# Threshold search of a sparse-attention layer: VectorE's three tiles in two streams in place of one

## The chip, the cores and the metric

The kernel runs on one core of one Trainium2 chip. The metric is device time in microseconds, taken as the median of repeated runs. A profile shows one execution, instruction by instruction. Its engines are PE (TensorE, matrix products), PEld (its weight loads), DVE (VectorE), ACT (ScalarE), POOL (GpSimd) and SP (SyncE, which issues the transfers).

## What is computed

The kernel is one decoder layer of width 1024 over 1024 tokens: a modulation of the input, one combined input projection, a mixer of sparse attention (8 heads) and causal pooling, a layer norm, and a gated feed-forward part with a second layer norm. The part that matters here is the choice of keys. An indexer gives each query a score for every earlier key, and the 256 keys of the highest score take part in that query's attention:

```
score = jnp.einsum('bqh,bqhs->bqs', w, jax.nn.relu(logits))
score = jnp.where(causal[None], score, -jnp.inf)
_, idx = lax.top_k(score, k_sel)              # k_sel = 256
...
s = jnp.where(valid[:, None], s, -jnp.inf)
p = jax.nn.softmax(s, axis=-1)
```

The queries are cut into eight tiles of 128. Tile i sees 128 (i + 1) keys, so tiles 0 and 1 take all of their keys and tiles 2 to 7 need a search for the 256th highest score.

## The kernel before

**The search.** Function `bisect` searches a list of tiles bit by bit. A score is cut into a high and a low half of 16 bits. For each of 15 bits of the high half and then 16 of the low half, a step counts, row by row, how many keys are at least a candidate, and then moves the candidate up or down by half of the last move. On VectorE (`search_v`) a step is one counting instruction per tile (a tensor_scalar that also writes out its sum; the trace calls it TENSOR_SCALAR_CACHE_REDUCE) and then two tiny instructions on one column per tile, which serve all tiles of the list at once:

```
for m, i in enumerate(tiles):
    dt = U16 if low else I16
    V.tensor_scalar(trash(i).bitcast(dt), kv[i].bitcast(dt), one(cand, m), one(base, m),
                    ALU.is_ge, ALU.add, accum_out=one(cntc, m))
V.tensor_scalar(pr, cntc, 0.0, float(1 << b), ALU.is_ge, ALU.mult)
off = -float(1 << (b - 1)) if b > 0 else -1.0
V.scalar_tensor_tensor(cand, pr, off, cand, ALU.add, ALU.add)
```

In this text these two are called the pair. Between the halves, each tile gets one more count (the keys above the high half) and a pass that builds its low keys; so a tile has 31 counts of the search and one more. After the low half each tile has a tail of passes: which keys equal the threshold, which lie below it, a scan that settles ties in order of position, and the write of the mask over the scores. `biased` then holds the tile. Tiles 4 and 3 in one list and tile 2 in another are searched by ScalarE (`search_a`, with Sign activations), with preparation and tail on VectorE. VectorE itself searches tiles 7, 6 and 5 in one list. Names in the trace: `keysD` and `keys` hold the keys, `junk` takes the counts' unused output, `colsD` the columns of VectorE's list, `colsA` those of ScalarE's.

**What sets the order.** `bisect` is a generator that yields, before each piece, the engine and a rough duration. While the projections are written out, the queues keep a clock of their own, and `fill` puts pieces of the search into an engine's queue ahead of an instruction of the main line that would otherwise leave that engine waiting by this clock; among the pieces that fit it takes the one that could start first. `need(i)` is called where attention needs tile i and advances the streams until it is masked. During the projections the order on VectorE, ScalarE and GpSimd is kept as written; after them (`pinned.clear()`) a scheduler decides, by its own estimates, what stands where on each engine.

**The stages around the change.** The index scores are accumulated on VectorE tile by tile (`score`). Then TensorE runs the pooling, key and value projections (`pair`, `pj` in the trace). Here VectorE has the search and besides it four subtractions for pooling (`u_split`, in the trace `ub<-ub,ub`; after them ScalarE writes `phi`, GpSimd `plo`, and TensorE multiplies, `po`), and eight pairs of writes of key operands (`kr<-kT`). GpSimd adds the pooling windows, rotates the keys (`rope`) and splits weights (`ws`). Then attention goes by groups of two query tiles: 7 and 6, 5 and 4, 3 and 2, 1 and 0. The query operands (`qab`) of tiles 7 and 6 are split once. For each pair of heads and each tile, a unit is: score products on TensorE (`s`), on VectorE a masked maximum per head that also adds the mask (`sm<-s,score`, CUSTOM_DVE_ANT_0 in the trace, ISA in the order below), exponentials on ScalarE, a reciprocal on VectorE (`stat`), the scaling on GpSimd (`sm<-sm,stat`), transposes on TensorE (`pT`), their copies on ScalarE and VectorE, and the products with the values (`o`). The weight blocks and the feed-forward part that follow are not touched.

Of the kernel before, what the change touches and what calls it, by code (L numbers as in the profile page):

```python
# [34 lines left out]
NEG = -3.0e38  # L35
NOT_TAKEN = -(2.0 ** 100)
TILES_A = [[4, 3], [2]]
TILES_V = [7, 6, 5]
PIN = "VAG"
AHEAD = 2  # L40
AHEAD_SMALL = 2
# [140 lines left out]
def decoder_layer_kernel(  # L182
# [8 lines left out]
    V, A, G, T, SP = (Queue(tc, e, n, pinned, times) for e, n in  # L191
                      ((nc.vector, "V"), (nc.scalar, "A"), (nc.gpsimd, "G"), (nc.tensor, "T"), (nc.sync, "S")))
# [13 lines left out]
    def buf(where, off, n, name, dt=F32):  # L206
        return nc.alloc_sbuf_tensor_at(f"{name}_{where}{off}", [P, n], dt, offset=area[where] + 4 * off).ap()
# [419 lines left out]
    def junkd(i):  # L627
        return junks.get(i, junk7)[:, 0 : P * (i + 1)]
# [4 lines left out]
    junkA = buf("T", 1664, 384, "junkA").bitcast(BF16)  # L633
    junkB = buf("X", 7360, 192, "junkB").bitcast(BF16)
    colsD = buf("X", 8576, 64, "colsD")
    keys = {2: kA[:, 0:192], 3: kA[:, 192:448], 4: k4, 5: k5, 6: kD[:, 0:448], 7: kD[:, 448:960]}
    keys = {i: kw.bitcast(I16) for i, kw in keys.items()}

# [2 lines left out]
    def bisect(tiles, cols, on_act):  # L641

        nt = len(tiles)
# [6 lines left out]
        def trash(i):  # L650
            return (ja if on_act else junkd(i))[:, 0 : P * (i + 1)]

        one = lambda c, m: c[:, m : m + 1]
        w_ = lambda i: (i + 1) / 8
# [17 lines left out]
        sum_w = sum(w_(i) for i in tiles)  # L672
# [13 lines left out]
        def search_a(bits, low):  # L686

            V.memset(cand, 0.5 - float(1 << (bits - 1)))
            for b in range(bits - 1, -1, -1):
                yield "A", 0.9 * sum_w + nt  # L690
                for m, i in enumerate(tiles):
                    A.activation(trash(i), kv[i].bitcast(U16 if low else I16), AF.Sign, bias=one(cand, m),
                                 accum_out=one(cntc, m))

                for m in range(nt):
                    A.activation(one(pr, m), one(cntc, m), AF.Sign, bias=one(thr, m))
                for m in range(nt):
                    A.activation(one(cand, m), one(pr, m), AF.Identity, scale=-0.5 * float(1 << b), bias=one(cand, m))
            yield "V", 0.1
            V.tensor_scalar(cand, cand, -1.0, None, ALU.mult)  # L700
# [40 lines left out]
    streams = []  # L741

    def open_stream(*a):
        pinned.update(PIN)
        b = bisect(*a)
        streams.append([T.t, next(b), b])
        times.fill = fill

    def start(st):
        return max(st[0], queues[st[1][0]].t)  # L750

    def advance(st):
        fill, times.fill = times.fill, None
        q = queues[st[1][0]]
        try:
            st[1] = next(st[2])
        except StopIteration:
            streams.remove(st)
        st[0] = q.t
        times.fill = fill  # L760

    def need(i):
        while i not in biased:
            advance(min(streams, key=start))

    def fill(q, until):
        while True:
            todo = [st for st in streams if st[1][0] == q.name and start(st) + st[1][1] <= until + SLACK.get(q.name, 0.0)]
            if not todo:
                return  # L770
            advance(min(todo, key=start))


    n_rr = [0]
# [12 lines left out]
    for i in range(2, NT):  # L787
# [27 lines left out]
                q_evac(*qpend.pop(0))  # L815
        dg = sc[:, n - P : n]
        G.affine_select(dg, dg, pattern=[[-1, P]], compare_op=ALU.is_ge, fill=NEG, base=0, channel_multiplier=1)
    open_stream(TILES_V, colsD, False)


    SP.dma_start(pscale, pscale_in)
# [309 lines left out]
    for n_, u in enumerate(units):  # L1131
        g, pr, i = u
# [162 lines left out]
    for p in range(NFP):  # L1295
# [7 lines left out]
        for kind in DOWN_AT if "d" in sets else "g" * 7 + "u" * 7:  # L1303
            w_ = names[kind].pop(0)
# [595 lines left out]
```

## Time and profile before

| | us |
|---|---|
| median of 3 runs (1322.52 to 1326.69) | 1326.66 |
| the profiled execution | 1332.07 |
| its span, first to last instruction | 1330.0 |
| PE, DVE busy over the span | 1197.3, 1071.2 |
| ACT, POOL busy over the span | 643.3, 734.5 |

The profiled execution is one run among others and lies 5.4 us above the median; a sum is made against its own time and carried over to the median. The shares over the whole span are means over stages with different limits, so the stages are read one by one, in the windows and in the engines' order of time. A row of the time line gives the start, the duration, the engine, the line (L169 is the helper through which every instruction goes), the operation, output<-inputs, shapes and the count of instructions; in brackets stands the idle time before it and what ended that.

### The profile page before, as it was taken

Reading aid. Unit: us, or ns where it says so; the run is one execution under the profiler, and the core shown is the slowest. Engines: PE = TensorE matmul, PEld = TensorE weight load, DVE = VectorE, ACT = ScalarE, POOL = GpSimd, SP = SyncE. Lnnn points to the kernel's source line nnn. Section 1 sums busy time; section 2 is a strip of 40 time slices with the busy share of each in tenths; the row PEclk is TensorE's granted clock in tenths of the full one; section 3 lists DMA queues with packets and bytes.
Section 4 is the critical chain, followed back from the end, with each engine's and each line's share of the span. In section 5 each row is a group of like instructions: output and inputs, shape, how many; then the busy total and the mean of one; then the engine's idle time right before and its main releaser. Section 6 shows DMA issues by size and latency. Waiting matters only on the chain.

```text
span 1330.0 us, 16034 instructions
## 1 busy us (share of the span) xinstructions
PE 1197.3 (90%) x5462; PEld 933.9 (70%) x5462; DVE 1071.2 (81%) x1755; ACT 643.3 (48%) x1335; POOL 734.5 (55%) x509
## 2 busy tenths in 40 slices
PE   7979998989258997999689999999999999999996
PEld 6646676768135654788577788878787887878775
DVE  6898999999996798466687787777868787777698
ACT  3345776868735776435544333333333333333431
POOL 1392496671013355327578384755748475666848
PEclk8999998989657998899899999999999999999998
DMA  9540021311000266320021101112020101113113
GB/s 338 222 160 26 17 95 51 109 48 40 16 0 10 70 216 238 123 92 9 32 96 33 64 32 65 55 40 80 32 80 32 64 33 64 64 42 117 41 61 121
DMA packets 34903, 103.90 MB, mean 78 GB/s; under 512 B 3843, under 2 KB 3843, under 8 KB 33286
## 3 DMA queue, kind: packets, MB, share of 16 engines
q1 hardware_dynamic: 34822, 102.88, 22.5%
q8 instruction: 43, 0.70, 0.2%
q14 instruction: 38, 0.31, 0.1%
HBM read 93.42 MB, written 9.45 MB: 77 GB/s over the span
## 4 chain that ended last, share of the span: by engine, by line
PE 55%; DVE 25%; POOL 7%; issue 6%; ACT 4%; DMA 2%; SPq 0%; DVEq 0%; POOLq 0%; ACTq 0%
PE gu L169 24%; PE dn L169 14%; DVE junk_X L169 4%; PE wo L169 4%; PE pj L169 3%; DVE score_X L169 3%; PE pT L169 2%; PE s L169 2%; PE o L169 2%; PE pair L169 2%; DVE act_W L169 2%; POOL wraw_R L169 1%; DVE utmp_X L169 1%; DVE stat_C L169 1%; DVE hr_H L169 1%
## 5 line engine op out<-in xcount | busy, mean ns | idle before, releaser
L169 PE MATMUL gu<-hr_H,wblk_T 128*128 128x512 f32 (+1 forms) x924 | 216.2, 385 | 4.7 <-POOL wblk_T L169 1.9
L169 PE MATMUL gu<-hr_H,wblk_V 128*128 128x512 f32 (+1 forms) x924 | 215.2, 384 | 3.7 <-POOL wblk_V L169 1.9
L169 PEld LDWEIGHTS gu<-hr_H,wblk_T 128*128 128x128 f32 x924 | 171.0, 189 | 41.3 <-POOL wblk_T L169 3.6
L169 PEld LDWEIGHTS gu<-hr_H,wblk_V 128*128 128x128 f32 x924 | 170.1, 188 | 40.0 <-POOL wblk_V L169 3.6
L169 DVE TENSOR_TENSOR res_X<-res_X,dn 128x512 f32<-128x512 f32 (+1 forms) x253 | 158.9, 677 | 15.4 <-PE dn L169 15.3
L169 POOL TENSOR_SCALAR sm_H<-sm_H,stat_X 128x1024 f32<-128x1024 f32 (+7 forms) x64 | 58.2, 921 | 164.8 <-DVE stat_X L169 142.7
L169 POOL TENSOR_TENSOR wraw_R<-wraw_R 128x512 f32<-128x512 f32 x64 | 94.7, 1486 | 47.0 <-DVE wblk_T L169 23.7
L169 PE MATMUL pj<-ws_W,hT_H 128*128 128x512 f32 x456 | 117.4, 404 | 2.5 <-DVE const_C L169 1.7
L169 POOL TENSOR_TENSOR wraw_W<-wraw_W 128x512 f32<-128x512 f32 x60 | 86.7, 1452 | 58.0 <-DVE wblk_V L169 29.3
L169 PEld LDWEIGHTS pj<-ws_W,hT_H 128*128 128x128 f32 x456 | 84.0, 190 | 27.6 <-issue 10.1
L169 PE MATMUL dn<-wblk_T,act_W 128*128 128x512 f32 x324 | 79.7, 395 | 4.7 <-DVE act_W L169 4.7
L169 PE MATMUL dn<-wblk_V,act_W 128*128 128x512 f32 x324 | 78.6, 391 | 2.9 <-DVE act_W L169 2.5
L169 DVE TENSOR_SCALAR_CACHE_REDUCE junk_X<-keysD_T,colsD_X 128x1024 int16<-128x1024 int16 (+1 forms) x64 | 79.0, 1270 | 0.9
L169 PEld LDWEIGHTS dn<-wblk_T,act_W 128*128 128x128 f32 x324 | 60.9, 189 | 19.4 <-DVE act_W L169 6.8
L169 ACT ACTIVATE wblk_V<-wraw_R 128x512 fp32r<-128x512 f32 x56 | 35.2, 629 | 80.7 <-POOL wraw_R L169 62.2
L169 PEld LDWEIGHTS dn<-wblk_V,act_W 128*128 128x128 f32 x324 | 60.4, 188 | 17.5 <-DVE act_W L169 4.2
L169 POOL TENSOR_TENSOR ws_W<-raw_R,ws_W 128x1024 fp32r<-128x1024 f32 x17 | 43.9, 2604 | 48.9 <-ACT ws_W L169 48.9
L169 ACT ACTIVATE wblk_V<-wraw_W 128x512 fp32r<-128x512 f32 x53 | 33.1, 627 | 75.0 <-POOL wraw_W L169 56.4
L169 ACT ACTIVATE wblk_T<-wraw_W 128x512 fp32r<-128x512 f32 x56 | 35.0, 628 | 66.3 <-POOL wraw_W L169 50.2
L169 ACT ACTIVATE sm_H<-sm_H,stat_X 128x1024 f32<-128x1024 f32 (+7 forms) x64 | 49.0, 768 | 34.0 <-DVE stat_X L169 34.0
L169 ACT ACTIVATE wblk_T<-wraw_R 128x512 fp32r<-128x512 f32 x52 | 32.5, 627 | 61.2 <-POOL wraw_R L169 45.8
L169 PE MATMUL pT<-const_C,sm_H 128*128 128x128 f32 x288 | 49.3, 308 | 10.9 <-POOL sm_H L169 6.4
(297 smaller groups left out, 2796.3 us busy)
## 6 DMA issues: line engine op xcount, KB each, us to landing
wm_K<-in_wma_dram SPq DMA_DIRECT2D x16, 512.0 KB, 9.6
modraw_V<-in_wmc_dram SPq DMA_DIRECT2D x16, 512.0 KB, 4.5
wraw_R<-in_wg_dram SPq DMA_DIRECT2D x6, 1024.0 KB, 4.8
wraw_R<-in_wd_dram SPq DMA_DIRECT2D x12, 512.0 KB, 3.5
wraw_W<-in_wup_dram SPq DMA_DIRECT2D x12, 512.0 KB, 3.5
modraw_V<-in_wmg_dram SPq DMA_DIRECT2D x10, 512.0 KB, 4.6
wraw_R<-in_wup_dram SPq DMA_DIRECT2D x10, 512.0 KB, 3.6
wraw_W<-in_wg_dram SPq DMA_DIRECT2D x5, 1024.0 KB, 4.8
```

The source lines that it names most:

```text
L169: ins_ = f(*a, **k)
```

## The change

VectorE's list becomes two: tiles 7 and 6 with the columns `colsD`, and tile 5 with columns of its own, `colsE`, in a place that was free. `fill` takes, among pieces that could start at the same time, the stream of the higher tile first; `need` advances the stream that holds the tile asked for, and no longer whichever could start first, so tile 5 has to be done only when attention asks for it. ScalarE's search is handed out count by count in place of step by step, with the same stated durations in sum; its instructions are the same.

```diff
--- before.py
+++ after.py
@@ -35,7 +35,7 @@
 NEG = -3.0e38
 NOT_TAKEN = -(2.0 ** 100)
 TILES_A = [[4, 3], [2]]
-TILES_V = [7, 6, 5]
+TILES_V = [[7, 6], [5]]
 PIN = "VAG"
 AHEAD = 2
 AHEAD_SMALL = 2
@@ -633,6 +633,7 @@
     junkA = buf("T", 1664, 384, "junkA").bitcast(BF16)
     junkB = buf("X", 7360, 192, "junkB").bitcast(BF16)
     colsD = buf("X", 8576, 64, "colsD")
+    colsE = buf("X", 5312, 64, "colsE")
     keys = {2: kA[:, 0:192], 3: kA[:, 192:448], 4: k4, 5: k5, 6: kD[:, 0:448], 7: kD[:, 448:960]}
     keys = {i: kw.bitcast(I16) for i, kw in keys.items()}
 
@@ -687,10 +688,11 @@
 
             V.memset(cand, 0.5 - float(1 << (bits - 1)))
             for b in range(bits - 1, -1, -1):
-                yield "A", 0.9 * sum_w + nt
                 for m, i in enumerate(tiles):
+                    yield "A", 0.9 * w_(i) + 0.45
                     A.activation(trash(i), kv[i].bitcast(U16 if low else I16), AF.Sign, bias=one(cand, m),
                                  accum_out=one(cntc, m))
+                yield "A", 0.55 * nt
 
                 for m in range(nt):
                     A.activation(one(pr, m), one(cntc, m), AF.Sign, bias=one(thr, m))
@@ -743,7 +745,7 @@
     def open_stream(*a):
         pinned.update(PIN)
         b = bisect(*a)
-        streams.append([T.t, next(b), b])
+        streams.append([T.t, next(b), b, a[0]])
         times.fill = fill
 
     def start(st):
@@ -761,14 +763,14 @@
 
     def need(i):
         while i not in biased:
-            advance(min(streams, key=start))
+            advance(next(st for st in streams if i in st[3]))
 
     def fill(q, until):
         while True:
             todo = [st for st in streams if st[1][0] == q.name and start(st) + st[1][1] <= until + SLACK.get(q.name, 0.0)]
             if not todo:
                 return
-            advance(min(todo, key=start))
+            advance(min(todo, key=lambda st: (start(st), -max(st[3]))))
 
 
     n_rr = [0]
@@ -815,7 +817,8 @@
                 q_evac(*qpend.pop(0))
         dg = sc[:, n - P : n]
         G.affine_select(dg, dg, pattern=[[-1, P]], compare_op=ALU.is_ge, fill=NEG, base=0, channel_multiplier=1)
-    open_stream(TILES_V, colsD, False)
+    for q, tiles in enumerate(TILES_V):
+        open_stream(tiles, (colsD, colsE)[q], False)
 
 
     SP.dma_start(pscale, pscale_in)
```

What this does to VectorE's queue, at three places. A counting instruction stands here as a TENSOR_SCALAR with two outputs, `junk` and the column.

In the projections, ahead of the subtraction for pooling, VectorE has whole steps of three tiles before:

```order
L169 TENSOR_SCALAR junk_X_607,colsD_X_615<-keysD_T_610,colsD_X_615 128x1024
L169 TENSOR_SCALAR junk_X_608,colsD_X_615<-keysD_T_610,colsD_X_615 128x896
L169 TENSOR_SCALAR junk_X_609,colsD_X_615<-keys_T_612,colsD_X_615 128x768
L169 TENSOR_SCALAR colsD_X_615<-colsD_X_615 128x3
L169 SCALAR_TENSOR_TENSOR colsD_X_615<-colsD_X_615 128x3
L169 SCALAR_TENSOR_TENSOR ub_V_1220<-ub_V_1220,ub_V_1221 128x1024
```

And in the changed kernel a step of two tiles, and one of tile 5 with a pair of its own:

```order
L169 TENSOR_SCALAR junk_X_607,colsD_X_615<-keysD_T_610,colsD_X_615 128x1024
L169 TENSOR_SCALAR junk_X_608,colsD_X_615<-keysD_T_610,colsD_X_615 128x896
L169 TENSOR_SCALAR colsD_X_615<-colsD_X_615 128x2
L169 SCALAR_TENSOR_TENSOR colsD_X_615<-colsD_X_615 128x2
L169 TENSOR_SCALAR junk_X_609,colsE_X_616<-keys_T_612,colsE_X_616 128x768
L169 TENSOR_SCALAR colsE_X_616<-colsE_X_616 128x1
L169 SCALAR_TENSOR_TENSOR colsE_X_616<-colsE_X_616 128x1
L169 SCALAR_TENSOR_TENSOR ub_V_1221<-ub_V_1221,ub_V_1222 128x1024
```

The step of tiles 7 and 6 has lost a count, and tile 5's step has a second pair. Up to the sixth pair of key writes, 17 pairs of tiny instructions stand before and 30 now.

Where attention starts, VectorE has before, from the first split of the query operands to the first maximum (`sm`):

```order
L169 TENSOR_TENSOR qab_H_2446<-qT_2453,qab_H_2446 64x512 x2
L169 TENSOR_SCALAR score_X_77<-score_X_77 128x1024
L169 TENSOR_SCALAR colsD_X_615<-colsD_X_615 128x1
L169 TENSOR_SCALAR keys_T_612<-score_X_77,colsD_X_615 128x768
L169 TENSOR_TENSOR qab_W_2447<-qT_2458,qab_W_2447 64x512 x2
L169 TENSOR_TENSOR keysD_T_610<-keysD_T_610,score_X_77 128x1024
L169 SCALAR_TENSOR_TENSOR score_X_77<-keysD_T_610,colsD_X_615 128x896
L169 TENSOR_TENSOR junk_X_607<-junk_X_607,keysD_T_610 128x1024
L169 TENSOR_SCALAR score_X_77<-score_X_77 128x896
L169 TENSOR_SCALAR score_X_77<-junk_X_607 128x1024
L169 TENSOR_TENSOR keysD_T_610<-keysD_T_610,score_X_77 128x896
L169 ISA sm_H_2445,stat_X_2440<-s_2509,score_X_77 128x1024
```

In the changed kernel, where tiles 7 and 6 are done by then:

```order
L169 TENSOR_SCALAR junk_X_609,colsE_X_616<-keys_T_612,colsE_X_616 128x768
L169 TENSOR_SCALAR colsE_X_616<-colsE_X_616 128x1
L169 SCALAR_TENSOR_TENSOR colsE_X_616<-colsE_X_616 128x1
L169 TENSOR_SCALAR junk_X_609,colsE_X_616<-keys_T_612,colsE_X_616 128x768
L169 TENSOR_TENSOR qab_H_2480<-qT_2487,qab_H_2480 64x512 x2
L169 ISA sm_H_2479,stat_X_2474<-s_2554,score_X_77 128x1024
L169 ISA stat_X_2474 128x1
L169 TENSOR_TENSOR qab_W_2481<-qT_2492,qab_W_2481 64x512 x2
L169 ISA sm_H_2479,stat_X_2474<-s_2555,score_X_77 128x1024
L169 ISA stat_X_2474 128x1
L169 ISA sm_H_2479,stat_X_2474<-s_2580,score_X_77 128x896
```

The split of qab_H stood among the passes of the tail; now it stands behind four low-half steps of tile 5, directly ahead of the first maximum, and the second split (qab_W) stands behind that maximum. 20 of tile 5's 32 counts are ahead of the first maximum, 12 behind it.

Once the first three units' six maxima are out, VectorE has before, up to the first maximum of the fourth unit, the following (the first row is the scan in tile 4's tail):

```order
L169 SCALAR_TENSOR_TENSOR score_X_77<-keys_T_611,colsA_X_606 128x640
L169 RECIPROCAL stat_X_2440<-stat_X_2440 128x2
L169 TENSOR_SCALAR score_X_77<-score_X_77 128x640
L169 TENSOR_TENSOR keys_T_611<-keys_T_611,score_X_77 128x640
L169 TENSOR_TENSOR junkA_T_613<-junkA_T_613,keys_T_611 128x640
L169 TENSOR_SCALAR score_X_77<-junkA_T_613 128x640
L169 TENSOR_SCALAR junkA_T_613,colsA_X_606<-score_X_77,colsA_X_606 128x512
L169 RECIPROCAL stat_X_2440<-stat_X_2440 128x2
L169 TENSOR_SCALAR colsA_X_606<-colsA_X_606 128x1
L169 SCALAR_TENSOR_TENSOR score_X_77<-keysA_X_605,colsA_X_606 128x512
L169 ISA sm_H_2445,stat_X_2440<-s_2742,score_X_77 128x896
```

In the changed kernel, from the fourth maximum (the last of the second unit) on:

```order
L169 ISA sm_H_2479,stat_X_2474<-s_2581,score_X_77 128x896
L169 ISA stat_X_2474 128x1
L169 RECIPROCAL stat_X_2474<-stat_X_2474 128x2
L169 ISA sm_H_2479,stat_X_2474<-s_2611,score_X_77 128x1024
L169 ISA stat_X_2474 128x1
L169 ISA sm_H_2479,stat_X_2474<-s_2612,score_X_77 128x1024
L169 ISA stat_X_2474 128x1
L169 TENSOR_SCALAR colsE_X_616<-colsE_X_616 128x1
L169 SCALAR_TENSOR_TENSOR colsE_X_616<-colsE_X_616 128x1
L169 TENSOR_SCALAR junk_X_609,colsE_X_616<-keys_T_612,colsE_X_616 128x768
L169 COPY pT_H_2476<-pT_2683 128x4x128
L169 RECIPROCAL stat_X_2474<-stat_X_2474 128x2
```

The first reciprocal stood behind the tails of tiles 5 and 4; now it follows the fourth maximum, and steps of tile 5 stand between the units.

On PE, in the group of tiles 7 and 6, some transposes stand ahead of score products that they stood behind; the instructions are the same. POOL and SP have the same order as before, and from the first maxima of tile 5 on, the passes that end tile 2 are the only difference on VectorE.

## Rows read from the trace of the kernel before

**Rows 1.** The page: the span, and TensorE's clock in tenths in 40 slices.

```profile
span 1330.0 us, 16034 instructions
...
PEclk8999998989657998899899999999999999999998
```

**Rows 2.** Busy us by stage (instructions), TensorE's clock, DMA share, GB/s.

```profile
170.60:375.40 204.80, 157.09 (x655) 124.78 (x653) 199.90 (x346) 148.67 (x416) 100.39 (x64) 0.87 0.18 57
375.40:436.10 60.70, 49.49 (x227) 31.37 (x228) 46.63 (x95) 34.04 (x74) 16.26 (x14) 0.70 0.03 6
187.00:303.00 116.00, 103.53 (x426) 82.93 (x425) 113.54 (x191) 85.03 (x224) 83.55 (x53) 0.93 0.22 69
411.00:416.00 5.00, 5.00 (x21) 3.00 (x22) 1.19 (x4) 1.19 (x2) 0.96 (x1) 0.57 0.00 0
416.00:421.00 5.00, 4.27 (x38) 2.92 (x33) 4.75 (x12) 2.15 (x5) 2.04 (x2) 1.00 0.00 0
435.00:450.00 15.00, 15.00 (x117) 10.28 (x117) 9.10 (x22) 12.60 (x28) 5.73 (x7) 1.00 0.08 19
```

**Rows 3.** VectorE in order of time (start us, us, instruction): one step.

```profile
329.14 1.34 DVE L169 TENSOR_SCALAR_CACHE_REDUCE junk_X<-keysD_T,colsD_X 128x1024 uint16<-128x1024 uint16 x1
...
331.53 1.07 DVE L169 TENSOR_SCALAR_CACHE_REDUCE junk_X<-keys_T,colsD_X 128x768 uint16<-128x768 uint16 x1
...
332.64 0.17 DVE L169 TENSOR_SCALAR colsD_X<-colsD_X 128x3 f32<-128x3 f32 x1
...
333.05 1.34 DVE L169 TENSOR_SCALAR_CACHE_REDUCE junk_X<-keysD_T,colsD_X 128x1024 uint16<-128x1024 uint16 x1
```

**Rows 4.** VectorE's groups: the pair, 187 to 303 and 303 to 360.4; a count.

```profile
L169 DVE SCALAR_TENSOR_TENSOR colsD_X<-colsD_X 128x3 f32<-128x3 f32 x17 | 17.1, 1007 | 0.6
...
L169 DVE TENSOR_SCALAR colsD_X<-colsD_X 128x3 f32<-128x3 f32 (+1 forms) x18 | 7.4, 411 | 0.6
...
L169 DVE TENSOR_SCALAR colsD_X<-colsD_X 128x3 f32<-128x3 f32 x14 | 2.4, 169 | 0.5
L169 DVE SCALAR_TENSOR_TENSOR colsD_X<-colsD_X 128x3 f32<-128x3 f32 x14 | 2.3, 163 | 0.5
...
230.28 1.33 DVE L169 TENSOR_SCALAR_CACHE_REDUCE junk_X<-keysD_T,colsD_X 128x1024 int16<-128x1024 int16 x1
```

**Rows 5.** VectorE's timeline: tiny instructions at the start of the search.

```profile
173.76 4.32 DVE L169 TENSOR_SCALAR colsD_X<-colsD_X 128x3 f32<-128x3 f32 x6
```

**Rows 6.** VectorE's timeline where attention starts, up to tile 5's first maximum.

```profile
366.83 1.38 DVE L169 TENSOR_TENSOR qab_H<-qT,qab_H 64x512 fp32r<-64x512 f32 x2
...
369.27 1.39 DVE L169 TENSOR_TENSOR qab_W<-qT,qab_W 64x512 fp32r<-64x512 f32 x2
...
375.43 1.22 DVE L169 CUSTOM_DVE_ANT_0 sm_H<-s,score_X 128x1024 f32<-128x1024 f32 x1
...
377.73 0.62 DVE L169 TENSOR_TENSOR junk_X<-junk_X,keysD_T 128x896 bf16<-128x896 bf16 x1
...
393.28 0.14 DVE L169 RECIPROCAL stat_X<-stat_X 128x2 f32<-128x2 f32 x1
...
399.87 1.06 DVE L169 CUSTOM_DVE_ANT_0 sm_H<-s,score_X 128x896 f32<-128x896 f32 x1
...
415.79 0.15 DVE L169 TENSOR_SCALAR colsA_X<-colsA_X 128x1 f32<-128x1 f32 x1
...
421.73 0.34 DVE L169 TENSOR_SCALAR score_X<-junkB_X 128x384 f32<-128x384 bf16 x1
...
436.12 0.96 DVE L169 CUSTOM_DVE_ANT_0 sm_H<-s,score_X 128x768 f32<-128x768 f32 x1 [0.89 <-PE s L169]
```

**Rows 7.** TensorE's timeline; in brackets idle us before, and what ended it.

```profile
207.61 0.74 PE L169 MATMUL po<-phi_V,wps_X 128*128 128x512 f32 x2 [1.97 <-ACT ub_V L169]
...
367.54 1.94 PE L169 MATMUL s<-kr_K,qab_H 64*128 64x512 f32 x4 [25.99 <-DVE qab_H L169]
376.81 3.90 PE L169 MATMUL s<-kr_K,qab_W 128*128 128x512 f32 x8 [7.33 <-DVE stat_X L169]
```

## Prediction

> **What bounds the kernel now.** I read the page first for the span and the row of TensorE's clock [rows 1], then the busy times by stage [rows 2], then the instructions of VectorE and TensorE around the point where attention starts [rows 3, 6, 7]. Between the last index score (170.6 us) and the first maximum of attention (375.4 us) VectorE is busy 199.90 of 204.80 us, while TensorE works for 157.09 of them [rows 2]. It has finished its projections and waits: its row at 367.54 stands behind 25.99 us of idle that ended with a VectorE split, and its clock falls to 0.5 of full speed in the slice from 366 to 399 us [rows 1, 7]. So up to 375.4 us the length is what VectorE has in its queue. After that the picture changes: from 375.4 to the first maximum of tile 5 at 436.1 VectorE is busy 46.63 of 60.70 us, and 14.1 us are free [rows 2, 6]. These free 14 us are what the change could fill, and the queue in front of 375.4 is what it has to shorten.
>
> One search step of three tiles takes 3.91 us, from 329.14 to 333.05: three counts, then a pair of tiny instructions of three columns each that move the candidates [rows 3]. Tile 5's count takes 1.11 of it until the pair starts, and the pair 0.41.
>
> **The change part by part.**
>
> *The steps before attention.* Each of the 31 search steps of tiles 7 and 6 loses tile 5's count. Some 0.1 us between the last count and the pair stays whichever count is last, so I take 1.0 of the 1.11 us: 31 x 1.0 = -31.0 us. But tile 5 needs its counts all the same, and the new order of VectorE has 20 of its 32 counts ahead of the first maximum (19 of the search, and the one that counts the keys above, which stood there before too), with 18 pairs of their own. 19 x 1.11 + 18 x 0.41 = +28.5 us. A pair of one column is priced as a pair of three, since its fixed part is nearly all of it. Three tiny instructions are added where a search begins, at 0.72 us each (4.32 for six, [rows 5]), and three at its middle, at 0.2: +2.8.
>
> *Collisions with GpSimd.* The pair is not always 0.41 us. Between 187 and 303 us, where GpSimd is busy 83.55 of 116 us, the mean of its second instruction is 1007 ns and of its first 411; between 303 and 360.4, where GpSimd is done, they are 163 and 169 [rows 2, 4]. That is 1.1 us more for a pair. A count does not suffer: 1.33 us at 230.28 as against 1.34 at 329.14 [rows 3, 4]. Up to the sixth pair of key writes into kr (behind it only two GpSimd ropes are left) the order has 17 pairs now and 30 in the changed kernel. If the same GpSimd work lies in a longer stretch, a pair meets it less often; I take 0.9 us a pair: 30 x 0.9 - 17 x 1.1 = +8.3. The bounds are 0 (each GpSimd instruction blocks VectorE once, however many pairs there are) and 13 x 1.1 = 14.3; I stay near the rows, which are pairs of the same kind beside the same GpSimd work.
> [...]
>
> *The edge of attention.* Two passes of the 0.62 us kind that end tile 6 now stand before the first maximum, one such pass of tile 5 and the second query split (1.39) stand behind it: -0.8 [rows 6]. The first query split, at 366.83 now with 8.6 us of tail work behind it, moves to directly before the first maximum. TensorE's four matmuls that wait for it took 1.94 us [rows 7]; now nothing on VectorE covers them: +2.0.
> Sum before the first maximum: -31.0 + 28.5 + 2.8 + 8.3 - 0.8 + 2.0 = +9.8 us (bounds +1.5 and +15.8).
>
> *From the first maximum to tile 5's.* VectorE's work there is 46.6 now. It gains tile 5's last 12 counts and 13 pairs, 12 x 1.11 + 13 x 0.41 = 18.6, and the 0.8 from the edge; it loses the tail of tile 2 (from 415.79 to 422.0, less a reciprocal and an output split among them: 5.8 us, [rows 6]), which moves behind tile 5's first maximum. 46.6 + 18.6 + 0.8 - 5.8 = 60.2. GpSimd is busy 16.26 of 60.70 us here, so 13 pairs meet it at about a third of the rate above: between 0 and 5, I take +2. And VectorE cannot run without gaps: after each two maxima the next wait for eight score matmuls of TensorE, 3.90 us at the low clock [rows 7], which tail passes cover now and which stand bare in the new order. Two such gaps of some 2.3 us and a short one make 5; the bounds are 0 and 12. Sum: 67.2 in place of 60.7, +6.5 (bounds -0.5 and +13).
>
> *Behind it.* Tile 2's 5.8 us now fall among the maxima of tile 5. VectorE has room there (9.10 of 15 us busy, [rows 2]), so I take +1, with bounds 0 and 5.8. From there on all five engines have the rows that they had.
>
> *What costs nothing.* The four u splits come later on VectorE, since more steps stand ahead of them; GpSimd, ScalarE and TensorE wait for them (TensorE waited 1.97 us at 207.61 already, [rows 7]). I expect TensorE's projections to end some 10 us later. Their cover is the 25.99 us for which it idles afterwards; if the delay were above it, the rest would count. ScalarE searches its tiles one count at a time now, and 10 more of its counts fall into attention, at about 1 us: it is busy 34.04 of 60.70 us there [rows 2], so they are covered. SP's and GpSimd's orders are the same, so no transfer is moved past another.
>
> Together +9.8 + 6.5 + 1 = +17.3 us. The profiled execution took 1332.07 us (span 1330.0 and 2.1 around it), which becomes 1349.4; it lay 5.4 above the median of 1326.66, so against that I forecast 1344.
>
> **The rivals.**
> *Faster.* In the present order the first reciprocal of attention stands at 393.28, 17.9 us behind the first maximum, and the fourth unit's first maximum at 399.87, because the ends of tiles 5, 4 and 3 are queued before them [rows 6]. The new order puts that reciprocal directly behind the fourth maximum, some 9 us after the first. If the group of tiles 7 and 6 is bound by this chain (reciprocal, GpSimd's scaling, transposes, products) rather than by the amount of VectorE's work, it shortens by those 9 us, to 52, in place of growing by 6.5. With the collisions at their lower bound the total is 1.5 - 9 = -7.5: 1319. It decides if the first maximum comes by 377 us and tile 5's by 430. For it: the 14.1 free us. Against it: 18.6 us of added work are more than 14.1.
> *No difference.* The tiny pairs do not collide more than now and the gaps fill: +1.5 before attention, -0.5 in it, +1 behind: +2, 1329.
> *Slower still.* TensorE stays at the low clock. At 411 to 416 us it works 5.00 of 5 us at 0.57, and from 416 on it has 1.00 [rows 2]; in the group its 49.49 busy us at a mean clock of 0.70 are 34.6 at full speed and 69 at half. If VectorE's searches feed it too thinly, the group lasts 69 and the 5 us of start, 74, or +13; with collisions at +14 before it the total is 15.8 + 13 + 1 = +30: 1357.
> [...]
> *The change does not do what it says*, that is tile 5 is searched before attention after all: 12 of its 32 counts stand behind the first maximum in the order, so this is excluded.
>
> **How the numbers follow.** The forecast, +17 give or take 9, gets 0.58; slower still 0.14; no difference 0.15; faster 0.13. What a measurement of this kernel can tell from no change is about 0.3%, 4 us. So faster by more than that 0.13, within it 0.15, slower 0.72. The range must keep 8 in 10: from 1328, which leaves out the faster case and some of the even one, to 1358, where collisions and clock are both at their bad ends.
>
> **What would show it.** In the profile of the changed kernel: a two-tile step of 2.9 us and a one-tile step of 1.5 where GpSimd is idle; pairs of one column at 0.15 to 0.2 us each; the mean of the pairs before 310 us at 0.9 us above that; the first maximum at 385 us (375.4 now), directly behind the first query split, with a wait for TensorE of about 2 us; tile 5's first maximum 67 us behind it, with VectorE busy over 60 of these. Wrong would be: a first maximum by 377 us, or a group of tiles 7 and 6 that lasts 55 us or less although VectorE does 18 us more in it, or a TensorE that ends its projections later than VectorE reaches the first query split.

## The result and the profile after

The changed kernel takes 1335.64 us (median of 4 runs, 1334.65 to 1336.61) beside 1326.68 for the kernel before, a ratio of 1.0073 with a 95% interval of 1.0050 to 1.0096. A second series gave 1336.95 beside 1327.28, 1.0070 (1.0049 to 1.0091). It is slower, by 9 us. The forecast had 17.

The page of the profiled execution of the changed kernel, its span and TensorE's clock (compare [rows 1]):

```profile
span 1332.9 us, 16110 instructions
...
PEclk8999998889867898999799999999999999999998
```

The spans differ by 2.9 us only, but the first profile of the kernel before lay 5.4 us above its own median. From the query split of the next group (468.91 us) to the output projection (540.99) it took 72.1 us; a second profile of the same kernel took 68.3, the changed kernel 67.4. So that second profile (`c0_before_again` below) is the one to compare with.

The stages of the changed kernel: busy us (instructions) of PE, PEld, DVE, ACT, POOL, then TensorE's clock, DMA share and GB/s. The first goes from VectorE's first count to the first maximum of attention, the second to tile 5's first maximum, the third to the next query split:

```profile
172.10:376.10 204.00, 160.52 (x655) 127.10 (x654) 198.10 (x366) 134.11 (x366) 101.21 (x64) 0.88 0.17 58
376.10:440.10 64.00, 50.76 (x224) 31.39 (x222) 56.25 (x135) 44.39 (x116) 16.35 (x14) 0.75 0.02 5
440.10:477.70 37.60, 35.05 (x238) 23.60 (x239) 29.87 (x71) 25.40 (x55) 13.88 (x14) 0.95 0.26 86
```

The same of the kernel before, second profile:

```profile
171.10:377.00 205.90, 157.92 (x655) 125.28 (x653) 201.12 (x346) 148.53 (x416) 101.14 (x64) 0.86 0.17 57
377.00:435.00 58.00, 46.67 (x227) 30.36 (x228) 46.65 (x95) 33.96 (x74) 16.28 (x14) 0.74 0.02 7
435.00:467.80 32.80, 32.70 (x233) 21.79 (x233) 24.68 (x57) 25.19 (x55) 13.98 (x14) 1.00 0.30 98
```

The stretch before attention, where the prediction saw most of the loss, has not become longer: 204.0 as against 205.9. The group of tiles 7 and 6 has (+6.0), and so has the stage behind it (+4.8).

VectorE's order of time in the changed kernel, from the first count to the next query split (compare [rows 6]; in brackets the idle us before, and what ended it):

```profile
172.10 1.22 DVE L169 TENSOR_SCALAR_CACHE_REDUCE junk_X<-score_X 128x1024 bf16<-128x1024 f32 x1 [1.46 <-POOL score_X L169]
...
374.11 1.40 DVE L169 TENSOR_TENSOR qab_H<-qT,qab_H 64x512 fp32r<-64x512 f32 x2
376.10 1.22 DVE L169 CUSTOM_DVE_ANT_0 sm_H<-s,score_X 128x1024 f32<-128x1024 f32 x1 [0.58 <-PE s L169]
...
383.25 0.16 DVE L169 RECIPROCAL stat_X<-stat_X 128x2 f32<-128x2 f32 x1
...
440.10 0.95 DVE L169 CUSTOM_DVE_ANT_0 sm_H<-s,score_X 128x768 f32<-128x768 f32 x1
...
441.85 0.15 DVE L169 TENSOR_SCALAR colsA_X<-colsA_X 128x1 f32<-128x1 f32 x1
...
448.65 0.36 DVE L169 TENSOR_SCALAR score_X<-junkB_X 128x384 f32<-128x384 bf16 x1
...
477.74 1.38 DVE L169 TENSOR_TENSOR qab_H<-qT,qab_H 64x512 fp32r<-64x512 f32 x2
```

The first query split stands directly before the first maximum, as forecast, but the wait between them is 0.58 us. The first reciprocal comes 7.2 us behind the first maximum (17.9 before, [rows 6]). Tile 2's tail, 441.85 to 449.01, lies among tile 5's maxima. TensorE ends its projections and waits 18.85 us in place of 25.99 [rows 7], so the later u splits stayed covered:

```profile
374.84 1.94 PE L169 MATMUL s<-kr_K,qab_H 64*128 64x512 f32 x4 [18.85 <-DVE qab_H L169]
```

### The profile page after: what moved, and what is told of

It is laid out like the page before. It is cut to its first block, busy times and chain, and to the rows that moved or that the text cites. A ratio compares the mean times of both kernels' runs of the same rounds, so it can differ in the third digit from the quotient of the medians.

```text
span 1332.9 us, 16110 instructions
## 1 busy us (share of the span) xinstructions
PE 1201.6 (90%) x5462; PEld 936.7 (70%) x5462; DVE 1081.6 (81%) x1828; ACT 640.0 (48%) x1335; POOL 737.4 (55%) x509
## 4 chain that ended last, share of the span: by engine, by line
PE 38%; DVE 6%; POOL 4%; issue 2%; ACT 1%; DVEq 0%; POOLq 0%; ACTq 0%
PE gu L169 24%; PE dn L169 14%; DVE act_W L169 2%; POOL wraw_R L169 1%; DVE utmp_X L169 1%; POOL wraw_W L169 1%; DVE gtmp_V L169 1%; POOL wblk_T L169 0%; DVE wblk_T L169 0%; DVE hr_H L169 0%; POOL hr_H L169 0%; DVE res_X L169 0%; DVE stat_C L169 0%; POOL wblk_V L169 0%; DVE wblk_V L169 0%
## 5 line engine op out<-in xcount | busy, mean ns | idle before, releaser
L169 PE MATMUL pj<-ws_W,hT_H 128*128 128x512 f32 x456 | 120.2, 411 | 6.4 <-ACT pout_K L169 2.7
L169 ACT ACTIVATE wblk_T<-wraw_R 128x512 fp32r<-128x512 f32 x52 | 32.5, 627 | 60.9 <-POOL wraw_R L169 45.5
```

Of the source, the lines that this page charges most:

```text
L169: ins_ = f(*a, **k)
```

## The experiments

Three theories were set against each other. **The split**: the loss is what VectorE's second stream adds (tiny instructions, their waits for GpSimd, counts inside attention). **The hand-out**: the change also makes ScalarE take its searches count by count and, through `need` and `fill`, orders the pieces differently, and the loss, or a gain that hides a larger loss, comes from there. **The tiny instructions**: whether a pair of one column meets GpSimd as one of three does, which the sum had assumed.

All runs in one table. The stages are those above; times of profiles in us, ratios to the kernel before, with 95% intervals.

| run | first count | to first maximum | to tile 5's | to next split | ratio |
|---|---|---|---|---|---|
| before, first profile | 170.62 | 204.81 | 60.69 | 32.79 | |
| c0: before again | 171.09 | 205.95 | 57.98 | 32.79 | 1.0010 (0.9992 to 1.0028) |
| changed kernel | 172.10 | 204.00 | 64.00 | 37.64 | 1.0073 (1.0050 to 1.0096) |
| c1: changed again | 174.54 | 203.55 | 64.45 | 37.63 | 1.0070 (1.0049 to 1.0091) |
| e8: changed, old hand-out | 170.11 | 206.31 | 64.03 | 41.56 | 1.0134 (1.0112 to 1.0156) |
| e1: changed, one stream | 172.46 | 205.51 | 46.64 | 32.91 | 0.9945 (0.9928 to 0.9963) |
| e6: before, new hand-out | 171.78 | 213.80 | 45.55 | 33.76 | 0.9980 (0.9965 to 0.9995) |
| e2: two pairs in the kernel before | 170.40 | 223.02 | 53.31 | 33.00 | 1.0084 (1.0052 to 1.0116) |
| e3: changed, one-column instructions | 172.12 | 182.94 | 75.03 | 34.70 | 0.9959 (0.9940 to 0.9978) |
| e7: one stream, one column, other order | 172.05 | 213.20 | 44.35 | 33.12 | 0.9985 (0.9969 to 1.0001) |
| e10: one stream, one column, e1's order | 173.49 | 196.95 | 46.67 | 32.89 | 0.9863 (0.9842 to 0.9885) |
| e11: two streams, one column | 172.42 | 185.87 | 65.14 | 34.92 | 0.9944 (0.9926 to 0.9963) |
| e9: changed, without tile 2's tail | 173.08 | 203.90 | 64.56 | 33.55 | 1.0073 (1.0047 to 1.0098) |

**Both kernels again.**

> The kernel before, unchanged, for a second profile. Every theory: the time of the kernel before, 1323 to 1328 us, the first maximum of attention at 375 to 376 us, the next query split behind tile 5's maxima at 468 to 470. If the loss of the change is made before attention's second group and then only carried along, the output projection here starts some 8 to 9 us earlier than in the changed kernel (545.2 there), at 536 to 537 us. If instead the late attention gives back what was lost, it starts at 541 again, as in the first profile.

The output projection starts at 536.09 us here and at 545.18 in the changed kernel: 9.1 us, which is the whole loss. What is lost up to the next query split is carried to the end.

> The changed kernel, unchanged, for a second profile and beside the runs above. Every theory: 1333 to 1337 us, first maximum at 375 to 377, tile 5's first maximum 64 us later, next query split at 477 to 478, output projection from 545 on.

The three stages repeat within 0.5 us; this execution's search began 2.4 us later, and its query split stands at 480.17.

**One stream again, the rest of the change kept** (against the changed kernel).

```diff
-TILES_V = [[7, 6], [5]]
+TILES_V = [[7, 6, 5]]
```

> The changed kernel with tiles 7, 6 and 5 in one stream again; what is left of the change is that ScalarE's searches are handed out one count at a time. If the loss comes from VectorE's second stream (tiny instructions, tile 2's tail): no loss, 1324 to 1329 us, first maximum at 375 to 376. If it comes from the finer hand-out on ScalarE and the other order it brings: 1333 to 1337 us.

Neither theory had this: the kernel is faster than the one before, 1316.40 us. The rows show where. VectorE's stages from the first maximum on, and its first reciprocal, in this run:

```profile
378.00:424.60 46.60, 40.91 (x227) 27.65 (x228) 43.56 (x95) 36.58 (x86) 17.28 (x14) 0.82 0.03 8
424.60:457.50 32.90, 32.80 (x235) 21.87 (x235) 24.77 (x57) 25.15 (x55) 14.02 (x14) 1.00 0.31 98
...
387.15 0.15 DVE L169 RECIPROCAL stat_X<-stat_X 128x2 f32<-128x2 f32 x1
```

and the same reciprocal in the kernel before, second profile:

```profile
394.88 0.14 DVE L169 RECIPROCAL stat_X<-stat_X 128x2 f32<-128x2 f32 x1
```

It comes 9.2 us behind the first maximum (377.97) in place of 17.8 (377.04), since the ends of tiles 5, 4 and 3 are no longer all queued ahead of it. The group lasts 46.6 us in place of 58.0, and VectorE's free time in it falls from 11.4 us to 3.0. So the rest of the change (count by count on ScalarE, `need`, and the choice in `fill` of the higher tile's stream), for which the prediction had no price, gains some 7 us in one stream.

**The hand-out on ScalarE alone, in the kernel before.**

```diff
-                yield "A", 0.9 * sum_w + nt
                 for m, i in enumerate(tiles):
+                    yield "A", 0.9 * w_(i) + 0.45
                     A.activation(...)
+                yield "A", 0.55 * nt
```

> The kernel before (one stream for tiles 7, 6 and 5) with ScalarE's searches handed out one count at a time, and nothing else; tails are still asked for as in the kernel before. In VectorE's order the first reciprocal stands 13 rows behind the first maximum (30 in the kernel before). Theory A (the finer hand-out alone spreads the tails of tiles 5, 4 and 3 over the gaps of attention's first group): group of tiles 7 and 6 of 47 to 50 us in place of 58 to 61, total 1315 to 1320. Theory B (it is the changed order in which tails are asked for that does it): group of 57 to 61, total 1323 to 1328.

1323.38 us, at the lower end of theory B's range in time, and the stages say why: the group is short (45.6 us), as theory A has it, but the first maximum comes 8 us later (213.8 us behind the first count), with 39 VectorE passes of ScalarE's tiles ahead of it in place of 19 (reads of accumulators not counted); the ends of tiles 4 and 3 are among them. e1 differs from this run in two rules, `need` and the choice in `fill`, and has 19. So the full gain needs count by count on ScalarE and one or both of these rules; no run parts the two.

**The change with ScalarE's old hand-out** (against the changed kernel).

```diff
-                    yield "A", 0.9 * w_(i) + 0.45
...
-                yield "A", 0.55 * nt
+                yield "A", 0.9 * sum_w + nt
```

> The changed kernel with ScalarE's old hand-out (a whole step at a time); the two VectorE streams stay. If the split costs some 17 us and the finer hand-out gives 7 to 8 of them back wherever it stands: 1341 to 1345 us. If the hand-out brings nothing beside the split, since VectorE's added work already fills the gaps of attention's first group: 1333 to 1337 us, with a group of 62 to 65 us.

1343.44 us: the split costs 17.9 us (1.34%), with the new `need` and `fill`, which this run keeps. The other way to it, the changed kernel against e1, gives 1.0073 / 0.9945 = 1.0129, some 17 us. The parts add up: 1.0134 x 0.9945 = 1.0078, and the whole change measured 1.0073 and 1.0070; but `need` and `fill` stand in both factors, and a run with the two streams alone, on the old rules, was not made. The loss lies behind the first maximum: 64.0 us for the group and 41.6 for the stage after it, where VectorE waits for ScalarE, which still searches, and then has the tails of tiles 4 and 3:

```profile
448.47 0.17 DVE L169 RECIPROCAL stat_X<-stat_X 128x2 f32<-128x2 f32 x1 [3.51 <-ACT sm_H L169]
449.92 0.69 DVE L169 TENSOR_SCALAR colsA_X<-colsA_X 128x2 f32<-128x2 f32 x1 [1.28 <-ACT colsA_X L169]
...
451.57 0.55 DVE L169 TENSOR_SCALAR keys_T<-score_X,colsA_X 128x640 bf16<-128x640 f32 x1
```

The first reciprocal comes early here too, 7.1 us behind the first maximum at 376.42, without the new hand-out:

```profile
383.56 0.16 DVE L169 RECIPROCAL stat_X<-stat_X 128x2 f32<-128x2 f32 x1
```

**A second pair in every step of the kernel before.**

```diff
-                V.tensor_scalar(pr, cntc, ...)
-                V.scalar_tensor_tensor(cand, pr, off, cand, ...)
+                for part in (slice(0, 2), slice(2, 3)):
+                    V.tensor_scalar(pr[:, part], cntc[:, part], ...)
+                    V.scalar_tensor_tensor(cand[:, part], pr[:, part], off, cand[:, part], ...)
```

> The kernel before, with tile 5's candidate moved by a pair of its own in every step: 31 pairs of one column more ahead of the first maximum, same counts. Theory 1 (a tiny instruction of one column does not wait for GpSimd, only those of several columns and some with two inputs do): some 20 pairs while GpSimd is busy at 0.57 us (0.15 and 0.42) and 11 at about 0.35, together +15 us: first maximum at 390 us, total 1341. Theory 2 (as on record: a pair of one column is blocked like one of three): 20 x 1.3 + 11 x 0.41 = +30: first maximum at 405, total 1356.

First maximum at 393.42, 1336.94 us in all (+0.84%): nearer to theory 1, and the rows say what is right in each. VectorE's groups between 172 and 312 us (busy us, mean ns of one, idle us before):

```profile
L169 DVE SCALAR_TENSOR_TENSOR colsD_X<-colsD_X 128x1 f32<-128x1 f32 x15 | 14.7, 978 | 0.5
L169 DVE SCALAR_TENSOR_TENSOR colsD_X<-colsD_X 128x2 f32<-128x2 f32 x15 | 12.7, 844 | 0.5
L169 DVE TENSOR_SCALAR colsD_X<-colsD_X 128x2 f32<-128x2 f32 x15 | 10.4, 695 | 0.0
...
L169 DVE TENSOR_SCALAR colsD_X<-colsD_X 128x1 f32<-128x1 f32 x18 | 2.4, 142 | 0.0
```

One column spares the first instruction of a pair (142 ns), not the second, which has two inputs (978). It also shows that further pairs bring further waits: all tiny instructions before the first maximum took 36.8 us above 0.17 us apiece, as against 22.8 in c0. I call this sum the waits for GpSimd below: in the profiles of the kernel before and the changed one, all 21 and 23 tiny instructions above 0.3 us ahead of the first maximum ended 0.01 to 0.03 us behind the end of a TENSOR_TENSOR of GpSimd.

**One-column, one-input instructions only.** Four or six short instructions take the place of a pair:

```diff
-                V.tensor_scalar(pr, cntc, ...)
-                V.scalar_tensor_tensor(cand, pr, off, cand, ...)
+                for m in range(nt):
+                    V.tensor_scalar(one(pr, m), one(cntc, m), ...)
+                for m in range(nt):
+                    V.tensor_scalar(one(cand, m), one(pr, m), one(cand, m), off, ...)
```

In the changed kernel, every step:

> The changed kernel, with each pair of tiny instructions replaced by one-input instructions of one column, two for each tile (four for tiles 7 and 6, two for tile 5). In the new order 4 of tile 5's steps more stand behind the first maximum. Theory 1 (one-column, one-input instructions do not wait for GpSimd): a two-tile step costs 4 x 0.17 = 0.7 us in place of 1.34 where GpSimd is busy (23 steps, -15) and of 0.41 where it is idle (8 steps, +2.5); with four steps of tile 5 less, -6, the first maximum comes some 18 us earlier, at 355 to 360, the group of tiles 7 and 6 is some 6 us longer, and the total is about 1322 to 1326. Theory 2 (all tiny instructions are blocked alike): the 46 added tiny instructions beside GpSimd cost up to 0.6 us each, +28: 1360.

1319.27 us, 16 below the changed kernel and somewhat below theory 1's range. From 172 to 312 us, with GpSimd busy for 101.53 of these 140 us, the 106 such instructions of tiles 7 and 6 show no waits (they overlap: 13.7 us in all, 0.13 for each, with a mean duration of 178 ns):

```profile
L169 DVE TENSOR_SCALAR colsD_X<-colsD_X 128x1 f32<-128x1 f32 x106 | 13.7, 178 | 0.0
```

The waits for GpSimd fall to 4.2 us. The first maximum comes at 355.06, and the group then lasts 75.0, since 16 of tile 5's counts stand in it now.

In one stream, for the 19 steps beside GpSimd:

> One stream for tiles 7, 6 and 5, ScalarE handed out count by count, and in the first 19 of 31 steps (those beside GpSimd) the pair of three columns is replaced by six one-column, one-input instructions. Theory 1 (these do not wait for GpSimd): 19 steps at 6 x 0.137 = 0.82 us in place of 1.3 to 1.4, -9 to -10 us: first maximum at 367 to 369, total 1306 to 1308 if attention's first group keeps its 46.6 us. Theory 2 (VectorE waits for GpSimd once for each GpSimd instruction, by whatever instruction comes first, or one-column instructions were spared by chance): no gain, 1316 or more.

1322.24 us: theory 2's time, but not by its mechanism. The instructions are short (7.0 us of waits for GpSimd in all), yet the planner, which prices each of them at 0.16 us, thought VectorE slow. It set 39 passes of ScalarE's tiles ahead of the first maximum, and u splits and key writes so early that VectorE waited for them: it is idle for 32.5 us from the first count to the next query split, in e1 for 13.5. Two of these rows:

```profile
220.93 3.35 DVE L169 SCALAR_TENSOR_TENSOR ub_V<-ub_V,ub_V 128x1024 f32<-128x1024 f32 x1 [3.80 <-POOL ub_V L169]
...
259.52 1.39 DVE L169 TENSOR_TENSOR kr_K<-kT,kr_K 64x512 fp32r<-64x512 f32 x2 [3.63 <-ACT kr_K L169]
```

The same, with the planner told the old price, so that everything else keeps e1's order:

> As e7_one_stream_one_column (one stream, fine hand-out, one-column one-input instructions in the first 19 steps), but with the order of all other instructions on VectorE exactly that of e1_one_stream; in e7 the planner had priced the six instructions too high and put the u splits and key writes so far forward that VectorE waited 32 us for them. If the instructions' durations decide (25 us of waiting for GpSimd in e1's tiny instructions against 7 in e7): first maximum 10 to 14 us before e1's 378, at 364 to 368, group of tiles 7 and 6 of 46 to 48 us, total 1303 to 1308. If VectorE's waits for GpSimd's u sums and ScalarE's key copies bind instead once VectorE is faster: first maximum at 372 or later, total 1311 or more.

1309.16 us, 1.4% below the kernel before: this beats both kernels. It lies between the two expectations, and there is something of each. VectorE's waits for GpSimd are 4.5 us as against e1's 22.9. Of the 18.4 us, 8.6 shorten the stretch before the first maximum (196.95 us for 205.51), because VectorE now catches up with what it needs and waits for that:

```profile
216.49 1.22 DVE L173 SCALAR_TENSOR_TENSOR ub_V<-ub_V,ub_V 128x1024 f32<-128x1024 f32 x1 [1.80 <-POOL ub_V L173]
...
292.79 1.39 DVE L173 TENSOR_TENSOR kr_K<-kT,kr_K 64x512 fp32r<-64x512 f32 x2 [4.62 <-ACT kr_K L173]
304.43 1.39 DVE L173 TENSOR_TENSOR kr_K<-kT,kr_K 64x512 fp32r<-64x512 f32 x2 [2.25 <-ACT kr_K L173]
```

And the split beside it, with the same instructions:

> The changed kernel (two VectorE streams, fine hand-out) with the same one-column instructions as e10_same_order_one_column in the steps beside GpSimd, priced so that VectorE's order stays nearly that of the changed kernel (a tile 5 count stands some rows later behind the first maximum). Beside e10 it is the split alone, without waits for GpSimd. If the split's loss of 17 to 19 us lies in the added tiny instructions' waits for GpSimd (29 us in the changed kernel, 22 in the kernel before): 7 us less than that, 1319 to 1321. If it lies behind the first maximum (group of tiles 7 and 6 of 64 us in place of 47, next query split 37 us behind it in place of 33, first maximum 1 to 3 us earlier than e10's): 1324 to 1329.

1316.65 us beside 1323.73 for the kernel before in the same series; at 1326.7 the ratio would make 1319, the first expectation. Beside e10 the split costs 0.9944 / 0.9863 = 1.0082, some 11 us, where it costs 17 to 18 with the old pairs in both. These 6 to 7 us are not the collisions of the added pairs alone. e11 is not free of waits for GpSimd: they are some 9 us, for e10's 4.5, as the edit leaves the last 12 steps of tiles 7 and 6 their pairs, and three of these instructions still met GpSimd (1.77, 2.30 and 1.22 us, from 285 us on). So the added waits are some 4.5 us here, and 6.6 in the changed kernel against e1 (29.5 and 22.9). The rest stands in another place: ahead of the first maximum VectorE is idle for 11.8 us in e10, where it waits for its inputs, and for 4.7 in e11. What remains of the loss is the group, 65.1 us with VectorE busy for 57.1, as against 46.7 and 43.6 in e10: tile 5's counts. The stages of e11 up to tile 5's first maximum, and those of e10:

```profile
172.40:358.30 185.90, 152.85 (x655) 121.80 (x654) 181.19 (x401) 134.32 (x366) 102.26 (x64) 0.92 0.20 64
358.30:423.40 65.10, 52.38 (x228) 32.33 (x226) 57.11 (x138) 44.89 (x116) 15.35 (x14) 0.74 0.01 5
```

```profile
173.50:370.40 196.90, 151.38 (x656) 121.13 (x654) 185.12 (x421) 141.42 (x396) 101.33 (x64) 0.90 0.19 61
370.40:417.10 46.70, 40.57 (x227) 27.26 (x228) 43.62 (x96) 36.60 (x86) 17.29 (x14) 0.83 0.04 8
```

**Without tile 2's tail.**

```diff
         for m, i in enumerate(tiles):
             ...
+            if i == 2:
+                biased.add(i)
+                return
             yield "V", 1.7 * w_(i) + 0.1
```

> The changed kernel without the tail of tile 2 (its mask is not computed and its scores are used in its place, so the output of these rows differs); on VectorE the tail lies among tile 5's maxima, in the stage up to the next query split (37.6 us long, 32.8 in the kernel before). If that stage has room for it, as forecast: that stage still 36 to 37.6 us and the total within 1 us of the changed kernel's. If it lies on the path: stage of 32.8, total 4 to 5 us below the changed kernel's, 1330 to 1331.

The stage is 33.55 us, 4.1 shorter, so it did not have room for the tail. The total is 1334.42, 1.2 to 2.5 us below the two series of the changed kernel, and the ratios are alike with intervals of 0.25% on either side. That the tail costs its 4 us at the end is neither shown nor excluded. In its own profile 1.3 us of them are gone again by the output projection (68.7 us behind the query split in place of 67.4), and the search had begun 1.0 us later.

## Why the prediction was right in sign and too large in size

**Its picture of the bound held.** VectorE's queue sets the time up to the first maximum, TensorE waits for the query split, and what is lost at the next query split is carried to the end. TensorE ended its projections 14 us later (355.99 us for 341.55, [rows 7]), and its idle time covered that, as forecast, though 10 us had been expected. Of the signs named, the first maximum (376.1 us, not 385) was wrong by most, and tile 5's first maximum (64.0 us behind it, not 67) by little. The prediction had said that a first maximum by 377 us would show it wrong, and this came about. That the total lies within its range is in part luck, since the sum put most of the loss in a stretch that lost nothing.

**A step that failed is the one on what costs nothing.** ScalarE's count by count was priced at 0 because ScalarE had free time, and the new `need` and `fill` got no term. Together they gain 7 us in one stream (e1 against the kernel before, 0.9945), and the hand-out alone gains 8 with two streams (the changed kernel against e8, 1.0073 against 1.0134). In one stream the mechanism stood in the text, as the rival that is faster: the first reciprocal comes early, and the group shortens by some 9 us. It shortens by 11 in e1 and 12 in e6, where the reciprocal stands 9.2 and 8.1 us behind the first maximum. With two streams this is not how the gain is made. The reciprocal comes 7.1 us behind the first maximum with the new hand-out and without it (e8), and the group lasts 64.0 us in both: an early reciprocal does not shorten the group once VectorE has the added work in it, which is where the rival was wrong. Of the 6.9 us between the profiled executions of e8 and the changed kernel (1341.55 and 1334.65), 4.3 lie ahead of the next query split: 2.3 before the first maximum and 3.9 in the stage behind the group, where the tails of tiles 4 and 3 no longer stand, less a search that begins 2.0 later. A small price of the same part was missed too: VectorE's first count waits 1.4 us for GpSimd's mask in the kernels with the fine hand-out and 0.40 in the others, where the last score passes before it wait 0.75 us each for ReLUs, between which ScalarE's counts now stand.

**The split was put at the right size, by other parts.** For the split (e8 against the kernel before) the forecast of +17.3 us and the measured +17.9 agree by luck, since the stages don't:

| | forecast | changed kernel against c0 | e8 against c0 |
|---|---|---|---|
| to the first maximum | +9.8 | -1.9 | +0.4 |
| to tile 5's first maximum | +6.5 | +6.0 | +6.1 |
| to the next query split | +1 | +4.8 | +8.8 |

*Before the first maximum*, term by term against the first profile of before (VectorE's time from the start of one instruction to the start of the next, summed by kind). The counts gave -9.3 us, forecast -9.9. The waits for GpSimd went from 21.9 to 29.5 us: +7.6, forecast +8.3. Both terms hold. The term that failed is the price of the tiny instructions without GpSimd, 7.4 + 2.8 = +10.2 in the sum: all tiny instructions together rose by 10.8 us, and without the waits by 3.2. The reason is in the rows. With two streams, one stream's tiny instruction stands beside the other's count, which does not need its result, and the next instruction starts at once. VectorE in the changed kernel, where GpSimd is idle:

```profile
336.55 0.17 DVE L169 TENSOR_SCALAR colsD_X<-colsD_X 128x2 f32<-128x2 f32 x1
336.76 0.16 DVE L169 SCALAR_TENSOR_TENSOR colsD_X<-colsD_X 128x2 f32<-128x2 f32 x1
336.83 1.07 DVE L169 TENSOR_SCALAR_CACHE_REDUCE junk_X<-keys_T,colsE_X 128x768 int16<-128x768 int16 x1
...
339.09 0.15 DVE L169 TENSOR_SCALAR colsE_X<-colsE_X 128x1 f32<-128x1 f32 x1
339.15 1.20 DVE L169 TENSOR_SCALAR_CACHE_REDUCE junk_X<-keysD_T,colsD_X 128x896 uint16<-128x896 uint16 x1
...
340.28 0.16 DVE L169 SCALAR_TENSOR_TENSOR colsE_X<-colsE_X 128x1 f32<-128x1 f32 x1
340.40 0.17 DVE L169 TENSOR_SCALAR colsD_X<-colsD_X 128x2 f32<-128x2 f32 x1
```

Tile 5's pair takes 0.06 and 0.12 us of VectorE's time here, 0.18 in place of 0.41 [rows 3], and the pair of tiles 7 and 6 0.28, since the count behind it is tile 5's. In the one stream each of the three steps (count, first and second of the pair) needs the result of the one before it: the starts of the pair and of the next count are 0.20 and 0.21 us apart (332.64, 332.84 and 333.05 in the kernel before), as against the 0.06 and 0.07 us after which a count follows a tiny instruction of the other stream here. The 0.41 is mostly that. It is not that one column is cheaper: where tile 5's steps stand alone in the same kernel, its pair takes 0.38 us again.

```profile
371.23 0.15 DVE L169 TENSOR_SCALAR colsE_X<-colsE_X 128x1 f32<-128x1 f32 x1
371.42 0.16 DVE L169 SCALAR_TENSOR_TENSOR colsE_X<-colsE_X 128x1 f32<-128x1 f32 x1
371.61 1.07 DVE L169 TENSOR_SCALAR_CACHE_REDUCE junk_X<-keys_T,colsE_X 128x768 uint16<-128x768 uint16 x1
```

The rest of the difference: ScalarE's tiles had 2.5 us less of their passes there, which I had not looked for, and the wait for TensorE behind the query split, priced at 2.0, added nothing (0.58 us of idle there, 0.57 in the kernel before elsewhere).

*The waits for GpSimd* were rightly sized, though the sum was too coarse: it took every tiny instruction of the added pairs to be blocked. Tile 5's first one is not; VectorE from 172 to 312 us in the changed kernel (min, median, max ns):

```profile
L169 DVE TENSOR_SCALAR colsE_X<-colsE_X x10: 142/153/154, 189.7 to 296.8; 128x1 f32<-128x1 f32 x9, 128x1 int16<-128x1 f32 x1
...
L169 DVE SCALAR_TENSOR_TENSOR colsE_X<-colsE_X x6: 159/160/1214, 208.9 to 297.0; 128x1 f32<-128x1 f32 x6
```

All ten stay at 0.14 to 0.15 us, seven of them with GpSimd at work in all or part of that time, while a step's same instruction on two columns reaches 2.03 us in the same profile. In e2, e3 and e10 it is the same for 18, 106 and 117 of them (means of 142, 178 and 174 ns). Two columns and three waited: from 172 to 312 us the mean was 683 ns for 24 of two columns in the changed kernel, and 545 ns for 21 of three in c0. Why the number of columns decides is not shown. The lower bound of the term, that GpSimd blocks once however many pairs there are, is excluded by e2 (36.8 us as against 22.8). What the term is worth at the end is not shown: with e10 and e11 the split costs 6 to 7 us less, but e11 keeps some 4.5 us of added waits, and e10's idle time enters too.

*The group of tiles 7 and 6* came out near the forecast, +6.0 for +6.5, with VectorE busy for 56.25 us and not over 60, and 7.8 us free where 5 had been put. Tile 5's 12 counts took 12.4 us and its tiny instructions 4.6. (The stage's upper bound of +13 does not follow from its terms: 60.2 with 5 and 12 on top is 16.5 above 60.7. The measured time lies below both.)

*Behind it* the +1 for tile 2's tail failed as a stage (+4.8); what of it reaches the end is open (e9).

**The rivals.** No difference and slower still are out: the clock in the group was 0.75, not the half that the latter needed, and the ratio's interval excludes 1. Faster is out for this kernel, though the first maximum came by the 377 us that it asked for: tile 5's came at 440, not by 430. It is true for a part of the change (e1).

## What to carry to other kernels

Price each part of a change apart, and most of all the one that "only" changes when work is handed out: here the gain was in the hand-out and the order, the loss in the headline, and the two hid each other in one number. The price of a step that is a chain of small dependent instructions can't be read from the rows of the single stream: tile 5's pair took 0.38 us of VectorE's time where its steps stood alone, and 0.18 beside a second, independent stream. When instructions become cheaper, tell the planner so, or it moves other work by the old prices (e7 and e10 differ in nothing else, and by 13 us in their medians).

## What the runs showed of the hardware

- A VectorE tensor_scalar of one column (128x1, fp32, no accumulator) took 178, 174 and 142 ns in the mean between 172 and 312 us, in 106, 117 and 18 instructions of three kernels (e3, e10, e2), with GpSimd busy for 101.53 of these 140 us in e3 and 99.79 in e2. Of two or three columns, it took up to 2.33 us in the changed kernel and 2.32 in e2.
- A two-input instruction waited at one column too: 15 of them had a mean of 978 ns in e2, and one took 0.16 us where GpSimd did nothing (340.28 us in the changed kernel).
- Back to back, one-column instructions of the first kind took 0.11 us each (117 of them, 12.4 us in e10), so six cost less beside GpSimd (0.63 to 0.65 us) than one pair of three columns did (1.4 us in the mean, [rows 4]).
